# The low parts of 58 feed-forward weight tiles: an adding DMA in place of a VectorE subtraction

## The chip, the core and the metric

One core of a Trainium2 chip runs the whole program. A core has TensorE (PE, matrix products; PEld is its weight load), VectorE (DVE), ScalarE (ACT), GpSimd (POOL) and SyncE (SP). The engines run side by side, each through its own list in order, and wait for each other on semaphores. Here SP and POOL issue nearly all DMAs, and one set of 16 DMA engines carries them.

The metric is the time of one execution on the device in microseconds (us). Smaller is better.

## The reference, cut to what matters

It is one decoder layer, on 512 prompt tokens and 8 sample tokens that share all weights, in float32:

```python
h = rms_norm(x, g_pre1) * (1 + scale1) + shift1
z = h @ w_in                                # q | k | v | g | u | a | gate_r | gate_c
# retention over q, k, v (4 heads) -> ret_out ; causal convolution of u * sigmoid(a) -> conv_out
mix = (sigmoid(gr) * ret_out + sigmoid(gc) * conv_out) @ w_out
x = x + gate1 * rms_norm(mix, g_post1)
h = rms_norm(x, g_pre2) * (1 + scale2) + shift2
x = x + gate2 * rms_norm((silu(h @ w_gate) * (h @ w_up)) @ w_down, g_post2)
```

The model width is 1024 and the feed-forward width 2816, which is 22 column blocks of 128. Next to `x` the layer returns the updated retention states: 8 samples x 4 heads, each state 512 KB.

## The kernel before, in words

Activations lie with the channels on the 128 partitions and the 520 tokens along the row. A product runs in two halves of 260 tokens ("sides" 0 and 1), into one accumulator tile `acc` in PSUM, of which there are two.

**High and low parts.** Each factor of a product is split in two float32r tiles: `hi`, the rounded value, and `lo`, what the rounding left over. Three products go into the accumulator: hi x hi, hi x lo, lo x hi. A weight tile of 128x1024 (a piece, class `Piece`) thus passes through three buffers: `raw`, loaded by SP (line 89), `hi`, a rounding copy on ACT (line 168), and `lo`, the subtraction raw - hi on DVE (line 137). In `gemm_pe` each of the 8 blocks of a piece has six matmuls of 260 columns: four with `hi`, then two with `lo`. So the first use of a piece's `lo` stands behind four matmuls of its item.

**Items and their order.** The program is a fixed list of items, each with its matmuls (`pe`), what follows them on ACT and DVE (`post`) and its pieces. `Ctx.run` walks the list and writes each engine's instructions in that order. While it writes item i, it also writes the split of the pieces of the next items, so many that their planned cost reaches 10 us (`SPLIT_AHEAD`): in the feed-forward stage with both sides these are the pieces of item i+2. The load of a piece is written two pieces ahead of that (`DMA_AHEAD`). On ACT the order of one step is therefore: split of item i+2, then `post` of item i.

**Feed-forward.** For each column block f there are two items, gate and up. The `post` of gate is a Silu on ACT from `acc`. The `post` of up is a multiplication on DVE from `acc`, then the split of the product into hi (ACT) and lo (DVE). Blocks 0 to 4 (`NLAG = 5`) run one side at a time, earlier. Blocks 5 to 21 run with both sides: 17 x 2 pieces. The down projection then has 8 output blocks with three pieces each (8, 8 and 6 blocks of 128): 24 pieces.

**State updates.** Between the feed-forward items stand the last updates of the sample states (`state_unit`). One update is: on POOL, the load of the state of two updates later (line 1099); on ACT, four scaled copies (line 165, `T<-T,vsm`); on DVE, one scalar-tensor-tensor (line 150); on POOL, the store of the state (`ret_s`, line 1092), which waits for DVE. POOL issues its DMAs strictly in its own order. In the stage with both sides one update comes after about every second item: first behind the up items, and from block 15 on behind the gate items. For some samples a 512 KB load of rows (line 672) stands with it.

**Buffers.** `raw`, `hi` and `lo` tiles, the states and the activations share 45 buffers ("T4"), which are taken again in the order in which they come free.

Of the kernel before, what the change touches and what calls it, by code (L numbers as in the profile page):

```python
# [9 lines left out]
F32R = mybir.dt.float32r  # L10
I32 = mybir.dt.int32
AF = mybir.ActivationFunctionType
ALU = mybir.AluOpType
AX = mybir.AxisListType
PSUM = bass.MemoryType.PSUM
DRAM = bass.MemoryType.DRAM

P = 128
D = 1024
KT = 8  # L20
# [10 lines left out]
NF = DFF // P  # L31
# [25 lines left out]

# order of the loads at the start, and of the items of the start and of the middle (">x" splits x's weights early)
LOADS = "x0 0.1 2.0 x1 x2 x3 2.1 2.2 1.0 2.3 A0 0.0 3.0 0.2 0.3 3.2 3.1 3.3 A1 B0 U0 1.2 1.1 1.3 U1 B1"
# [9 lines left out]
NLAG = 5  # L69


class Item:
# [3 lines left out]
    def __init__(self, pe, post=None, pieces=(), cost=0.0, pre=None):  # L76
        self.pe, self.post, self.pieces, self.cost, self.pre = pe, post, list(pieces), cost, pre


class Piece:  # L80
    def __init__(self, k, src, shape, split=True):
        self.k, self.src, self.shape, self.want_split = k, src, list(shape), split
        self.raw = self.hi = self.lo = None

# [6 lines left out]
    def split(self):  # L91
        if self.want_split:
            self.hi, self.lo = self.k.split(self.raw, self.shape, late=self.k.late_w)
            self.raw = None
# [185 lines left out]
def halves(ap2d):  # L280
    return ap2d.rearrange("p (a b) -> p a b", a=2)


def emit(k, ins, outs):
# [21 lines left out]

    # modulation: quarters of the rows accumulate in four column groups of the array
    def ada_item(blk, n=2):
# [178 lines left out]
    items = []  # L487

    # start: modulation of the first norm, statistics of x
    ada = {b: ada_item(b, 1) for b in range(4)}  # L490
# [3 lines left out]

    # conv branch
    scv = k.sm([P, KT, NB], "scv")
    glu = {}
    conv = {}
# [64 lines left out]
    for j in range(KT):  # L563
# [24 lines left out]
        if j == 0:  # L588
            start = {f"{b}.{i}": it for b in range(4) for i, it in enumerate(ada[b])}
# [23 lines left out]

    # retention heads
    cos, sin = halves(csn[:, 0, :]), halves(csn[:, 1, :])
# [316 lines left out]

    # the last head's state product waits in DRAM for the end of the kernel
    def park(h):
        d = hd[h]
        kept = []
        for q in list(d["kd"]) + [q for p in range(2) for q in d["V"][p]]:
            kept.append(k._t(k.dram, [P, 4 * DK], F32R, f"park{len(kept)}"))
            nc.gpsimd.dma_start(kept[-1], q.rearrange("p a b -> p (a b)"))

        def back():
            t = []
            for i, q in enumerate(kept):
                t.append(k.t4([P, 4, DK] if i < 2 else [P, 2, DV], F32R))
                nc.gpsimd.dma_start(t[-1].rearrange("p a b -> p (a b)"), q)
            d["kd"], d["V"] = t[:2], {0: t[2:4], 1: t[4:6]}
        box["back"] = back
# [46 lines left out]

    # layer norm of the conv branch
    def ln_mean():
# [82 lines left out]

    # update of the sample states  # L1080
    def state_unit(h, b):
# [38 lines left out]

    # gates of the branches, merge
    sgr = {}
# [16 lines left out]
    last = []  # L1139
# [36 lines left out]

    # output projection, second norm
    MX = {}
# [163 lines left out]

    # feed-forward
    ACT = {}
# [25 lines left out]

    fpc = [(Piece(k, ins["w_gate"][f], [P, KT, P]), Piece(k, ins["w_up"][f], [P, KT, P])) for f in range(NF)]
    for a in range(2):
# [44 lines left out]
    def down_pieces(m):  # L1417
        return [Piece(k, ins["w_down"][m][:, 8 * i:min(NF, 8 * i + 8), :], [P, min(8, NF - 8 * i), P])
                for i in range(3)]
# [6 lines left out]
    def final(a):  # L1426
# [16 lines left out]
        return post  # L1443

    dp = [down_pieces(m) for m in range(KT)]
    items.append(Item(gains2))
    for m in range(KT - 2):
# [98 lines left out]
```

## Time and profile before

| what | value |
|---|---|
| time, median of 2 runs | 1189.4 us (1189.3 to 1189.51) |
| profiled execution: span from first to last instruction | 1188.2 us |
| what lies around the span (median less span) | 1.2 us |
| PE busy | 1165.3 us, 98% |
| DVE / ACT / POOL busy | 764.9 / 425.4 / 85.2 us |
| mean DMA rate over the span | 166 GB/s |
| granted TensorE clock, mean | 0.998 |

The profile page has no time of its own for the profiled execution besides its span. A line such as "L137 DVE" names the line of the kernel on which the instruction is recorded; many operations are recorded in one helper, so tiles and shapes tell them apart. "Idle before" is the time an engine stood still just ahead of an instruction, with what ended it. In a timeline the columns are: start, duration, engine, line, operation, tiles with sizes, count, and in brackets the idle time before. Busy time of PE is modelled, so it is read together with the chain of waits.

### The profile page before, as it was taken

The page shows a single profiled execution, that of the slowest core. Times are in us where ns is not written, and L with a number is a line of the kernel's source. Part 1 is how long each engine was busy: PE and PEld are TensorE (multiplying, and loading weights), DVE is VectorE, ACT ScalarE, POOL GpSimd, SP SyncE. Part 2 cuts the span into 40 slices and gives each one's busy share as a digit, 9 for nine tenths or more (in the row PEclk, how much of TensorE's full clock was granted, in tenths as well). Part 3 has the DMA queues.
Part 4 walks back from the last instruction along what each step waited for, and adds up shares of the span by engine and source line. Part 5 has one row for each costly group of instructions (what it writes and reads, how often), then busy time and mean ns, then how long its engine had stood idle before and what let it go on. Part 6 is the DMA issues. An engine that isn't in the chain of part 4 may idle for free.

```text
span 1188.2 us, 22500 instructions
## 1 busy us (share of the span) xinstructions
PE 1165.3 (98%) x9460; PEld 1128.4 (95%) x9460; DVE 764.9 (64%) x1475; ACT 425.4 (36%) x701; POOL 85.2 (7%) x153
## 2 busy tenths in 40 slices
PE   5999999999999999999999999999999999999997
PEld 2999999999999999999989999999999999999996
DVE  4697798999798989896545536685344443432224
ACT  3421233343233232334336335563344444332210
POOL 0000020011001100110000110100011111000000
PEclk9999999999999999999999999999999999999999
DMA  9821252244225432567554645634575564462224
GB/s 378 353 92 56 74 205 91 88 161 169 72 90 173 156 106 72 195 227 270 213 201 165 230 166 179 226 125 143 207 253 195 183 223 172 165 200 82 84 67 143
DMA packets 56885, 197.48 MB, mean 166 GB/s; under 512 B 6544, under 2 KB 8848, under 8 KB 56784
## 3 DMA queue, kind: packets, MB, share of 16 engines
q1 hardware_dynamic: 37008, 125.89, 30.2%
q0 software_dynamic: 19632, 70.12, 16.9%
q8 instruction: 74, 1.21, 0.4%
q14 instruction: 27, 0.22, 0.1%
q10 hardware_dynamic: 144, 0.04, 0.0%
HBM read 171.65 MB, written 25.32 MB: 166 GB/s over the span
## 4 chain that ended last, share of the span: by engine, by line
PE 97%; DVE 1%; DMA 1%; ACT 0%; SPq 0%; issue 0%; DVEq 0%
PE acc L207 88%; PE ps L207 7%; DVE T L137 1%; DMA T<-xT 1%; PE ps L958 1%; PE ps L844 1%; PE ps L329 0%; DVE T L150 0%; PE ps L785 0%; ACT T L165 0%; PE ps L658 0%; ACT T L168 0%; SPq L89 0%; DVEq L1542 0%; DVE ada_r L336 0%
## 5 line engine op out<-in xcount | busy, mean ns | idle before, releaser
L207 PE MATMUL acc<-T,T 128*128 128x260 f32 x8592 | 1055.8, 284 | 1.0 <-DVE T L137 0.5
L207 PEld LDWEIGHTS acc<-T,T 128*128 128x128 f32 x8592 | 1040.1, 188 | 12.0 <-issue 3.4
L137 DVE TENSOR_TENSOR T<-T,T 128x1024 fp32r<-128x1024 f32 (+8 forms) x343 | 328.2, 984 | 121.0 <-ACT T L168 77.6
L168 ACT CAST T<-T 128x1024 fp32r<-128x1024 f32 (+7 forms) x255 | 227.6, 927 | 257.2 <-DVE T L137 245.8
L137 DVE TENSOR_TENSOR T<-acc,T 128x520 f32<-128x520 f32 (+1 forms) x99 | 64.9, 669 | 158.9 <-PE acc L207 155.0
L150 DVE SCALAR_TENSOR_TENSOR T<-T,vec,T 128x511 f32<-128x511 f32 (+14 forms) x240 | 161.6, 729 | 0.0
L165 ACT ACTIVATE T<-acc 128x520 f32<-128x520 f32 (+1 forms) x98 | 50.3, 514 | 219.0 <-PE acc L207 219.0
L150 DVE SCALAR_TENSOR_TENSOR T<-T,T 128x1024 f32<-128x1024 f32 x32 | 39.2, 1225 | 53.3 <-ACT T L165 52.1
L165 ACT ACTIVATE T<-acc,GT 128x260 f32<-128x260 f32 (+1 forms) x32 | 15.2, 475 | 110.5 <-PE acc L207 100.3
L165 ACT ACTIVATE T<-T,vsm 128x256 f32<-128x256 f32 x128 | 54.2, 499 | 0.0
L207 PE MATMUL ps<-T,T 128*128 128x512 f32 (+3 forms) x264 | 51.8, 349 | 0.0
L168 ACT COPY T<-acc 128x520 f32<-128x520 f32 (+2 forms) x46 | 22.1, 481 | 73.8 <-PE acc L207 73.8
L207 PEld LDWEIGHTS ps<-T,T 128*128 128x128 f32 x264 | 42.5, 188 | 5.9
L692 DVE CUSTOM_DVE_ANT_0 T<-T,T 128x256 f32<-128x256 f32 x128 | 45.6, 419 | 0.0
L207 PE MATMUL ps<-T,cs 128*32 128x512 f32 x192 | 29.0, 647 | 11.4 <-DMA T<-w_ada 11.4
L1092 POOL DMA_DIRECT2D ret_s<-T x32 | 17.2, 537 | 255.1 <-DVE T L150 234.8
L207 PEld LDWEIGHTS ps<-T,cs 128*32 128x32 f32 x192 | 5.3, 112 | 21.5 <-issue 15.7
L137 DVE TENSOR_TENSOR T<-ps,T 128x512 fp32r<-128x512 f32 (+4 forms) x32 | 18.6, 585 | 9.3 <-ACT T L168 7.8
L150 DVE SCALAR_TENSOR_TENSOR T<-ps,vec,T 128x256 fp32r<-128x256 f32 (+1 forms) x32 | 18.5, 611 | 8.3 <-PE ps L958 7.6
L1099 POOL DMA_DIRECT2D T<-sret x32 | 16.9, 530 | 96.3 <-PE acc L207 73.2
L165 ACT ACTIVATE T<-ps,gn_b,gn_n 128x512 f32<-128x512 f32 x16 | 11.1, 779 | 32.1 <-DVE gn_b L150 23.1
L672 POOL DMA_DIRECT2D T<-rows x16 | 12.3, 770 | 142.1 <-PE acc L207 120.4
(110 smaller groups left out, 342.6 us busy)
## 6 DMA issues: line engine op xcount, KB each, us to landing
T<-w_in SPq DMA_DIRECT2D x77, 512.0 KB, 3.7
T<-sret POOLq DMA_DIRECT2D x64, 512.0 KB, 5.6
T<-w_ada SPq DMA_DIRECT2D x48, 512.0 KB, 5.4
ret_s<-T POOLq DMA_DIRECT2D x32, 512.0 KB, 4.4
T<-w_up SPq DMA_DIRECT2D x22, 512.0 KB, 4.5
T<-w_gate SPq DMA_DIRECT2D x22, 512.0 KB, 4.3
T<-rows POOLq DMA_DIRECT2D x16, 512.0 KB, 5.2
T<-w_ret_out SPq DMA_DIRECT2D x16, 512.0 KB, 3.5
```

The lines of the kernel that those rows point to most:

```text
L137: self.nc.vector.tensor_tensor(out=out, in0=a, in1=b, op=op)
L150: self.nc.vector.scalar_tensor_tensor(out=out, in0=a, scalar=s, in1=b, op0=op0, op1=op1)
L165: self.nc.scalar.activation(out, a, func, **kw)
L168: self.nc.scalar.copy(out, a)
L207: self.nc.tensor.matmul(out, lhsT=w, rhs=x, start=start, stop=stop)
L672: nc.gpsimd.dma_start(t, qk_rows[h][4 * g:4 * g + 4, i, :].unsqueeze(0).to_broadcast([P, 4, DK]))
L692: nc.vector.tensor_tensor_reduce(out=junk, in0=s0[b][:, vt, :], in1=d["qb", b // 4][:, b % 4, :], op0=ALU.mult, op1=ALU.add, scale=1.0, sc ...
L844: nc.tensor.transpose(t[:, vt * P:(vt + 1) * P], d["v"][vt // 2][:, vt % 2, jt * P:(jt + 1) * P], ident)
L958: nc.tensor.transpose(t[:, it * P:(it + 1) * P], d["y"][it // 2][:, it % 2, vt * P:(vt + 1) * P], ident)
L1092: nc.gpsimd.dma_start(outs["ret_s"][h, b], s0)
L1099: nc.gpsimd.dma_start(box2["s0"], ins["sret"][h, b])
```

## The change

A piece can now be marked `summed`. This mark is set on the gate and up pieces of blocks 5 to 21 (34) and on all 24 pieces of the down projection: 58. For such a piece ACT first writes -raw into `lo`, rounded to float32r, then the rounded copy into `hi`; then POOL issues a DMA that reads the same weights from DRAM once more and adds them onto `lo`. `lo` then holds raw less its rounded value. The subtraction on DVE is gone for these pieces. All other pieces stay as they are.

```diff
 class Piece:
-    def __init__(self, k, src, shape, split=True):
+    def __init__(self, k, src, shape, split=True, summed=False):
         self.k, self.src, self.shape, self.want_split = k, src, list(shape), split
+        self.summed = summed
         self.raw = self.hi = self.lo = None
...
     def split(self):
-        if self.want_split:
+        if self.summed:
+
+            k = self.k
+            self.hi, self.lo = k.t4(self.shape, F32R), k.t4(self.shape, F32R)
+            k.act(self.lo, self.raw, AF.Copy, scale=-1.0)
+            k.copy(self.hi, self.raw)
+            k.nc.gpsimd.dma_start(self.lo, self.src, accum_op=ALU.add)
+            self.raw = None
+        elif self.want_split:
             self.hi, self.lo = self.k.split(self.raw, self.shape, late=self.k.late_w)
             self.raw = None
...
-    fpc = [(Piece(k, ins["w_gate"][f], [P, KT, P]), Piece(k, ins["w_up"][f], [P, KT, P])) for f in range(NF)]
+    fpc = [tuple(Piece(k, ins[w][f], [P, KT, P], summed=f >= NLAG) for w in ("w_gate", "w_up")) for f in range(NF)]
...
-        return [Piece(k, ins["w_down"][m][:, 8 * i:min(NF, 8 * i + 8), :], [P, min(8, NF - 8 * i), P])
+        return [Piece(k, ins["w_down"][m][:, 8 * i:min(NF, 8 * i + 8), :], [P, min(8, NF - 8 * i), P], summed=True)
                 for i in range(3)]
```

The rest of the diff takes comments out. Lines behind line 100 stand 9 later in the changed kernel. PE's and SP's lists keep their order. On POOL, at the updates that stand near blocks 10 to 12 of the feed-forward, the list was this before (`T4_...` are buffers, those of `sret` and `ret_s` hold states):

```order
L1099 DMA T4_1427_10682<-sret 128x1024
L1092 DMA ret_s<-T4_1402_10430 128x1024
L1099 DMA T4_1438_10806<-sret 128x1024
L1092 DMA ret_s<-T4_1414_10556 128x1024
L1099 DMA T4_1451_10932<-sret 128x1024
L1092 DMA ret_s<-T4_1427_10682 128x1024
```

The same place on POOL in the changed kernel, where line 99 is the adding DMA:

```order
L1108 DMA T4_1427_10696<-sret 128x1024
L1101 DMA ret_s<-T4_1402_10440 128x1024
L99 DMA T4_1431_10708<-w_gate 128x1024
L99 DMA T4_1436_10766<-w_up 128x1024
L1108 DMA T4_1438_10822<-sret 128x1024
L1101 DMA ret_s<-T4_1414_10568 128x1024
L99 DMA T4_1442_10834<-w_gate 128x1024
L99 DMA T4_1447_10892<-w_up 128x1024
L1108 DMA T4_1451_10950<-sret 128x1024
L1101 DMA ret_s<-T4_1427_10696 128x1024
```

Between the store of one update and the load of the next now stand two adds, and the add of a gate piece is right behind a store. Further on, from block 16, where the update follows the gate item, it is the add of an up piece that stands right behind the store.

On ACT the list at the same blocks was this before (`vsm` marks the scaled copies of an update, an `acc` source the Silu, a `T2` source the hi part of the product):

```order
L165 ACTIVATE T4_1428_10684<-T4_1373_10161,vsm_40_146 128x256 x4
L168 CAST T4_1430_10693<-T4_1416_10565 128x1024
L165 ACTIVATE T2_1433_10745<-acc_1432_10696 128x520
L168 CAST T4_1435_10750<-T4_1421_10622 128x1024
L168 CAST T4_1425_10676<-T2_1433_10745 128x520
L165 ACTIVATE T4_1439_10808<-T4_1413_10554,vsm_40_146 128x256 x4
```

And on ACT after:

```order
L174 ACTIVATE T4_1428_10698<-T4_1373_10167,vsm_40_146 128x256 x4
L174 ACTIVATE T4_1431_10708<-T4_1416_10577 128x1024
L177 CAST T4_1430_10707<-T4_1416_10577 128x1024
L174 ACTIVATE T2_1433_10761<-acc_1432_10712 128x520
L174 ACTIVATE T4_1436_10766<-T4_1421_10635 128x1024
L177 CAST T4_1435_10765<-T4_1421_10635 128x1024
L177 CAST T4_1425_10691<-T2_1433_10761 128x520
L174 ACTIVATE T4_1439_10824<-T4_1413_10566,vsm_40_146 128x256 x4
```

Each weight's rounding copy has a negating copy of the same size ahead of it; nothing else moved on ACT.

## The prediction

> **What bounds the kernel now.** I read the page's busy times and its chain first, then the chain in order of time, the busy time by stage, and at last the timeline of one step of the stage that the change touches.
>
> ```profile
> span 1188.2 us, 22500 instructions
> PE 1165.3 (98%) x9460; PEld 1128.4 (95%) x9460; DVE 764.9 (64%) x1475; ACT 425.4 (36%) x701; POOL 85.2 (7%) x153
> PE 97%; DVE 1%; DMA 1%; ACT 0%; SPq 0%; issue 0%; DVEq 0%
> L207 PE MATMUL acc<-T,T 128*128 128x260 f32 x8592 | 1055.8, 284 | 1.0 <-DVE T L137 0.5 <-DVE T L150 0.4
> ```
>
> PE carries 97% of the chain. The last row is the group of all large products: ahead of 8592 matmuls PE stood 1.0 us in all, half of it for the line on which the removed subtractions stand. The chain in order of time (start, length, what) shows where the changed pieces are used:
>
> ```profile
> 877.84 280.32 PE acc L207 x2340
> ```
>
> For 280 us PE waits for nobody. The changed pieces of blocks 5 to 21 and the whole down projection lie in this stretch and the 27 us ahead of it. By stage (length, busy time of PE, PEld, DVE, ACT, POOL, clock, DMA share, GB/s), with the start of the program as the row of the highest DMA rate:
>
> ```profile
> 862.00:1045.00 183.00, 183.00 (x1528) 182.02 (x1527) 77.86 (x84) 77.70 (x135) 22.06 (x40) 1.00 0.58 197
> 1045.00:1159.00 114.00, 114.00 (x959) 114.00 (x958) 31.33 (x34) 31.66 (x61) 2.78 (x6) 1.00 0.33 105
> ...
> 0.00:30.00 30.00, 17.06 (x84) 6.88 (x84) 13.31 (x38) 10.34 (x15) 1.44 (x6) 1.00 0.96 379
> ```
>
> DVE, from which the work is taken, is busy 78 of 183 us in the gate/up stage and 31 of 114 in the down stage. So the question is not what DVE saves but whether the new path to `lo` is still in time for PE.
>
> **The change part by part.**
>
> *Removed: 58 subtractions.* The groups by shape, in the stretch from 850 to 1132 us (a piece of 6 blocks is 128x768):
>
> ```profile
> L137 DVE TENSOR_TENSOR T<-T,T 128x1024 fp32r<-128x1024 f32 x47 | 56.8, 1219 | 9.5 <-ACT T L168 6.4 <-issue 3.1
> L137 DVE TENSOR_TENSOR T<-T,T 128x768 fp32r<-128x768 f32 x7 | 6.7, 957 | 48.0 <-ACT T L168 48.0
> L168 ACT CAST T<-T 128x1024 fp32r<-128x1024 f32 x47 | 48.6, 1050 | 1.4 <-PE acc L207 0.9 <-DVE T L137 0.4
> ```
>
> 50 x 1.219 + 8 x 0.957 = 68.6 us leave DVE. None of it is on the chain: the 1.0 us of PE's idle time above is all that could come back, and it is spread over the whole kernel. I take 0.
>
> *Added on ACT: 58 negating copies.* Not shown as such; the nearest row is the rounding copy of the same tile, 1.05 us. In the gate/up stage ACT rises from 78 to about 78 + 34 x 1.05 = 113 of 183 us. One step shows what stands behind it (start, duration, engine):
>
> ```profile
> 906.74 0.70 DVE L137 TENSOR_TENSOR T<-acc,T 128x520 f32<-128x520 f32 x1 [6.22 <-PE acc L207]
> 907.35 1.82 DVE L137 TENSOR_TENSOR T<-T,T 128x1024 fp32r<-128x1024 f32 x2
> 907.47 0.63 ACT L168 CAST T<-T 128x520 fp32r<-128x520 f32 x1 [5.03 <-DVE T L137]
> 908.00 1.71 ACT L165 ACTIVATE T<-T,vsm 128x256 f32<-128x256 f32 x4
> ...
> 909.62 1.03 ACT L168 CAST T<-T 128x1024 fp32r<-128x1024 f32 x1
> 909.75 1.23 DVE L150 SCALAR_TENSOR_TENSOR T<-T,T 128x1024 f32<-128x1024 f32 x1 [0.57 <-ACT T L165]
> 910.89 1.22 DVE L137 TENSOR_TENSOR T<-T,T 128x1024 fp32r<-128x1024 f32 x1
> 911.26 0.54 POOL L1092 DMA_DIRECT2D ret_s<-T  x1 [9.78 <-DVE T L150]
> 911.80 0.53 POOL L1099 DMA_DIRECT2D T<-sret  x1
> ...
> 912.44 0.60 ACT L165 ACTIVATE T<-acc 128x520 f32<-128x520 f32 x1 [1.79 <-PE acc L207]
> ...
> 918.26 0.70 DVE L137 TENSOR_TENSOR T<-acc,T 128x520 f32<-128x520 f32 x1 [6.16 <-PE acc L207]
> ```
>
> An up item ends at 906.74 and the next one at 918.26: 11.52 us for two items, 5.76 each, 0.12 a matmul. The copy at 909.62 is that of the gate piece used from 918.26 on. With a negation ahead of it, ACT is done at 909.62 + 2 x 1.04 = 911.7, before the Silu at 912.44; nothing is late. The negation behind the Silu ends near 914, and ACT has nothing more to do before 919. So ACT's part costs 0; its cover is the 1.79 us of idle time ahead of the Silu, of which 1.05 go.
>
> *Moved: the end of `lo`.* Before, `lo` of that gate piece was done by the subtraction at 910.89 + 1.22 = 912.1, 6.1 us ahead of PE. Now the add is issued by POOL, and there the order of the list counts: it stands behind the store `ret_s`, which waits for DVE's update and so is issued at 911.26 to 911.80. What is queued behind the add on POOL is the up piece's add and the next state's load; that load is needed two updates later and has room. From the end of the up item the add begins at 911.80 - 906.74 = 5.06 us. It has to land 11.52 us after that end, plus the four matmuls that need only `hi`: 11.52 + 0.48 = 12.0. That leaves 6.94 us from issue to landing. Seven gate pieces in a row (blocks 10 to 16) stand like this.
>
> From block 15 on the update follows the gate item:
>
> ```profile
> 1015.95 0.60 ACT L165 ACTIVATE T<-acc 128x520 f32<-128x520 f32 x1 [3.40 <-PE acc L207]
> 1016.45 1.69 ACT L165 ACTIVATE T<-T,vsm 128x256 f32<-128x256 f32 x4
> ...
> 1018.17 1.23 DVE L150 SCALAR_TENSOR_TENSOR T<-T,T 128x1024 f32<-128x1024 f32 x1 [4.37 <-ACT T L165]
> 1019.69 0.54 POOL L1092 DMA_DIRECT2D ret_s<-T  x1 [6.82 <-DVE T L150]
> ...
> 1027.46 0.60 ACT L165 ACTIVATE T<-acc 128x520 f32<-128x520 f32 x1 [3.42 <-PE acc L207]
> ```
>
> The gate item ends at 1015.95, the store's issue at 1020.23, so the add of an up piece begins after 4.28 us and has 12.0 - 4.28 = 7.72. Six up pieces and the first middle piece of the down projection: seven. The last update follows the last up item, and behind its store stands one more down piece, with the gate pieces' 6.94. Adds without a store ahead start 2 to 3 us earlier and have 9 us and more. Blocks 6 to 9 have stores too, but there PE has other work of about a microsecond between items; I count them at 0.
>
> *The price of the add, A.* No adding DMA is in the trace. The nearest row is the state load: POOL's queue, 512 KB from DRAM, issued right behind the same store. Its landings in this stage, what POOL's queue moved there (packets, MB, share of the 16 engines over 183 us), and POOL's issue times, for the row load (more descriptors) and the state load:
>
> ```profile
> L1099 POOL DMA_DIRECT2D T<-sret x17: 528/528/531, 862.5 to 1023.9; - x17
> ...
> DMA to landing us min/median/max: 3.6/6.3/8.8
> ...
> q0 software_dynamic: 5616, 20.45, 31.7%
> ...
> L1099 POOL DMA_DIRECT2D T<-sret x17 | 9.0, 529 | 13.7 <-DVE T L137 7.2 <-DMA ret_s<-T 5.2 <-PE acc L207 0.9
> L672 POOL DMA_DIRECT2D T<-rows x4 | 3.0, 761 | 1.7 <-PE acc L207 1.7
> ```
>
> Low end: 3.6, the fastest load. High end: twice the median, 12.6, as if the read of the old `lo` were a second load behind the first. I take the median and one more pass over 512 KB: 0.317 x 183 = 58 us for 20.45 MB is 1.5 us for 0.524 MB, so A = 6.3 + 1.5 = 7.8. POOL's issue may take 0.76 instead of 0.53 us; I add 0.23 to the start of each.
>
> *The sum.* A stall ahead of one piece also gives the next add that much more time, so in a row of pieces half of the excess stays. Gates and the last down piece: 8 x (0.23 + 7.8 - 6.94) / 2 = 4.4 us. Ups: 7 x (0.23 + 7.8 - 7.72) / 2 = 1.1. Together 5.5. With A = 3.6 it is 0; with the largest state load, 8.8, it is 8 x 1.05 + 7 x 0.66 = 13; with 12.6 it is 8 x 2.95 + 7 x 2.56 = 41.
>
> *The rest of the down stage.* The copies of three pieces stand behind each output block's five evacuations:
>
> ```profile
> 1060.59 0.48 ACT L165 ACTIVATE T<-acc,GT 128x260 f32<-128x260 f32 x1 [10.25 <-issue]
> ...
> 1061.90 2.76 ACT L168 CAST T<-T 128x768 fp32r<-128x768 f32 x3
> 1062.80 3.31 DVE L137 TENSOR_TENSOR T<-T,T 128x768 fp32r<-128x768 f32 x3 [10.55 <-ACT T L168]
> ...
> 1076.34 0.48 ACT L165 ACTIVATE T<-acc,GT 128x260 f32<-128x260 f32 x1 [11.68 <-PE acc L207]
> ```
>
> Of the 15.75 us from one block to the next, the first of the three is used after 2 x 5.76 = 11.5 us. Its add is issued near 1062.9 and would land at 1070.7, needed at 1072.1; the two others have more. Cost 0.
>
> The span of the profiled execution is 1188.2, the median of the runs 1189.4, so 1.2 us lie around it. 1188.2 + 5.5 + 1.2 = 1194.9: I say 1195.
>
> **The rivals.** The line for a difference that a measurement of this kernel is taken to tell is 2%, 23.8 us.
>
> *The add is slow (slower).* One mechanism, at the gate and up pieces behind a store: with A from issue to landing the stall is 4 x (A - 6.71) + 3.5 x (A - 7.49), which reaches 23.8 at A = 10.2. For it: the read of the old tile, the rounding at the end, and a store of 512 KB just ahead in the same queue. Against it: the slowest of 17 loads in this place took 8.8. At A = 12.6 the time is 1189.4 + 41 = 1230.
>
> *The DMA engines fill up (slower).* In the stage they are busy 0.58. Two adds per 11.52 us at 1.5 us each are 0.26, at two passes each 0.52, so 0.84 or 1.10; in the latter case the 183 us stretch by 10%, 18 us and what the waits add: 1207 to 1215. Against it: 197 GB/s plus 2 x 0.524 MB / 11.52 us = 91 is 288, below the 379 of the start. [...]
>
> *PE gains (faster).* Only 1.0 us of PE's waiting for DVE is there in the products, so the best is 1188.4. That the subtractions stay, or are replaced by other work on DVE, is excluded: the built program has 58 fewer of them there.
>
> **How the numbers follow.** The forecast (A between 3.6 and 9, 1189 to 1203): 0.66. The slow add: 0.20, of which 0.12 over 23.8 us. Full DMA engines: 0.12, of which 0.07 over it. Faster: 0.02, and over 2% 0.01 at most. The range from 1187.5 to 1216 leaves out the outer part of the two slower rivals, about 0.16, and little below. Slower by over 2%: 0.19; faster 0.01; within 2%: 0.80.
>
> **What would show it.** Right: PE idle ahead of some `acc` matmuls, put down to the DMAs of `w_gate` and `w_up` and no longer to none; landings of the adds near 8 us; DVE lower by 69 us, ACT higher by 60; the span from 1045 us on longer by nothing. Wrong: landings above 10, a DMA share near 1 between 862 and 1045, waits of PE for pieces of the down projection, or a Silu that waits for ACT's negations and so keeps an accumulator from PE.

## The result, and the profile after

The changed kernel takes 1217.36 us (median of 2 runs, 1215.03 to 1219.69) against 1189.4 before: a ratio of 1.0234, with a 95% interval of 1.021 to 1.0259. It is slower by 28 us, where 5.5 us were forecast, and it lies just above the upper end of the range, 1216.

The page of the kernel after has these lines (span, busy times, queues, memory traffic, shares of the chain, the group of all large products):

```profile
span 1217.9 us, 22596 instructions
PE 1175.0 (96%) x9460; PEld 1135.6 (93%) x9460; DVE 701.3 (58%) x1417; ACT 478.7 (39%) x759; POOL 136.6 (11%) x211
q0 software_dynamic: 27984, 99.48, 29.6%
HBM read 201.01 MB, written 25.32 MB: 186 GB/s over the span
PE 77%; issue 13%; DMA 4%; POOL 3%; DVE 2%; ACT 1%; SPq 0%; POOLq 0%; DVEq 0%
L216 PE MATMUL acc<-T,T 128*128 128x260 f32 x8592 | 1065.5, 285 | 21.5 <-DMA T<-w_up 8.2
```

The work moved as it was meant to: DVE is 64 us lower, ACT 53 higher, and the 29.4 MB of the 58 weights are read a second time. The last line says where the time went, in two parts. PE stands still for 21.5 us ahead of the large products, where it was 1.0. And the same 8592 matmuls take 1065.5 us, where they took 1055.8. That is 20.5 + 9.7 = 30.2 us, and the span has grown by 29.7.

The stalls one by one (PE's timeline after; start, length of the run of matmuls that follows, in brackets the idle time ahead of it and what ended it):

```profile
869.81 7.93 PE L216 MATMUL acc<-T,T 128*128 128x260 f32 x44 [4.67 <-DMA T<-w_up]
892.56 6.01 PE L216 MATMUL acc<-T,T 128*128 128x260 f32 x48 [1.22 <-DMA T<-w_gate]
900.85 17.50 PE L216 MATMUL acc<-T,T 128*128 128x260 f32 x144 [2.27 <-DMA T<-w_up]
920.52 23.32 PE L216 MATMUL acc<-T,T 128*128 128x260 f32 x192 [2.18 <-DMA T<-w_gate]
944.57 11.78 PE L216 MATMUL acc<-T,T 128*128 128x260 f32 x96 [0.73 <-DMA T<-w_gate]
958.65 23.24 PE L216 MATMUL acc<-T,T 128*128 128x260 f32 x192 [2.30 <-DMA T<-w_gate]
983.65 19.06 PE L216 MATMUL acc<-T,T 128*128 128x260 f32 x144 [1.77 <-DMA T<-w_gate]
1003.20 23.33 PE L216 MATMUL acc<-T,T 128*128 128x260 f32 x192 [0.48 <-DMA T<-w_up]
1026.95 23.31 PE L216 MATMUL acc<-T,T 128*128 128x260 f32 x192 [0.43 <-DMA T<-w_up]
1050.62 23.31 PE L216 MATMUL acc<-T,T 128*128 128x260 f32 x192 [0.35 <-DMA T<-w_up]
1077.89 110.08 PE L216 MATMUL acc<-T,T 128*128 128x260 f32 x896 [3.96 <-DMA T<-w_down]
```

They add up to 20.4 us and fall into four places. Up to 901 us, on the up piece of block 6 and both pieces of block 8: 4.67 + 1.22 + 2.27 = 8.2. Four of the seven gates behind a store, those of blocks 10, 12, 13 and 15: 2.18 + 0.73 + 2.30 + 1.77 = 7.0; a stall gives the next add more time. Every second of the six ups behind a store, blocks 16, 18 and 20: 1.3. And 3.96 on the first middle piece of the down projection. From there on PE runs 110 us without a stop.

The second part, the slower matmuls, is seen in windows of 2 us behind a stall (length, PE busy and matmuls, PEld, DVE, ACT, POOL, granted clock, DMA share, GB/s):

```profile
870.00:872.00 2.00, 2.00 (x10) 2.00 (x11) 0.00 (x0) 0.21 (x1) 2.00 (x4) 0.50 0.94 295
872.00:874.00 2.00, 2.00 (x11) 2.00 (x11) 0.00 (x0) 0.00 (x0) 0.63 (x2) 0.50 1.07 283
874.00:876.00 2.00, 2.00 (x14) 2.00 (x13) 0.00 (x0) 0.00 (x0) 0.00 (x0) 0.71 1.03 299
876.00:878.00 2.00, 2.00 (x19) 1.69 (x21) 0.23 (x1) 0.00 (x0) 0.00 (x0) 1.00 1.07 379
```

PE is as busy as before, but for 6 us it does 10 to 14 matmuls in 2 us where 19 are usual: the granted clock is 0.50 to 0.71. Behind the stall that ends at 1077.89 it is the same; behind the one that ends at 983.65 it is so for 4 us. (The share of the DMA engines, the column behind the clock, can read a little over 1 in a short window, here up to 1.07.)

The stage rows show the engines that the adds pass through (the same columns; the adds' landing time stands below):

```profile
862.00:1045.00 183.00, 166.95 (x1341) 164.09 (x1340) 41.45 (x50) 98.00 (x154) 47.69 (x68) 0.97 0.96 271
1072.00:1186.00 114.00, 110.04 (x897) 109.83 (x897) 4.10 (x8) 47.12 (x77) 20.91 (x26) 0.97 0.82 188
```

```profile
DMA to landing us min/median/max: 4.8/7.6/13.7
```

The share of the DMA engines has gone from 0.58 to 0.96. The adds' median of 7.6 us is what the forecast took (7.8); their spread reaches 13.7.

### The profile page after: what moved, and what is told of

The parts are those of the page before. It is cut to its first block, busy times and chain, and to the rows that moved or that the text cites. A ratio compares the mean times of both kernels' runs of the same rounds, so it can differ in the third digit from the quotient of the medians.

```text
span 1217.9 us, 22596 instructions
## 1 busy us (share of the span) xinstructions
PE 1175.0 (96%) x9460; PEld 1135.6 (93%) x9460; DVE 701.3 (58%) x1417; ACT 478.7 (39%) x759; POOL 136.6 (11%) x211
## 3 DMA queue, kind: packets, MB, share of 16 engines
q1 hardware_dynamic: 37008, 125.89, 29.6%
q0 software_dynamic: 27984, 99.48, 29.6%
## 4 chain that ended last, share of the span: by engine, by line
PE 77%; issue 13%; DMA 4%; POOL 3%; DVE 2%; ACT 1%; SPq 0%; POOLq 0%; DVEq 0%
PE acc L216 68%; PE ps L216 7%; POOL T L99 1%; DVE T L146 1%; POOL T L1108 1%; DMA T<-w_down 1%; DMA T<-sret 1%; DMA T<-w_gate 1%; DVE T L159 1%; DMA T<-w_up 1%; PE ps L967 1%; PE ps L853 1%; DMA T<-xT 1%; POOL ret_s L1101 1%; ACT T L174 0%
## 5 line engine op out<-in xcount | busy, mean ns | idle before, releaser
L216 PE MATMUL acc<-T,T 128*128 128x260 f32 x8592 | 1065.5, 285 | 21.5 <-DMA T<-w_up 8.2
L146 DVE TENSOR_TENSOR T<-T,T 128x1024 fp32r<-128x1024 f32 (+10 forms) x285 | 262.4, 944 | 153.0 <-ACT T L174 116.5
L174 ACT ACTIVATE T<-T 128x1024 fp32r<-128x1024 f32 (+3 forms) x74 | 73.6, 996 | 14.3 <-DVE T L146 11.7
L99 POOL DMA_DIRECT2D T<-w_down x24 | 20.4, 864 | 87.4 <-ACT T L174 87.4
L99 POOL DMA_DIRECT2D T<-w_gate x17 | 15.0, 884 | 107.0 <-ACT T L174 106.2
L1108 POOL DMA_DIRECT2D T<-sret x32 | 23.2, 737 | 11.6 <-DVE T L146 10.2
```

The costliest lines, as they stand in the source:

```text
L99: k.nc.gpsimd.dma_start(self.lo, self.src, accum_op=ALU.add)
L146: self.nc.vector.tensor_tensor(out=out, in0=a, in1=b, op=op)
L174: self.nc.scalar.activation(out, a, func, **kw)
L216: self.nc.tensor.matmul(out, lhsT=w, rhs=x, start=start, stop=stop)
L1108: nc.gpsimd.dma_start(box2["s0"], ins["sret"][h, b])
```

## The experiments

Two theories stand against each other. *Position* (P): an add is issued so late in its place, behind a store on POOL, that it has about 7 us until PE needs it, and takes about that long. *Full engines* (F): the 16 DMA engines are at their limit, and everything that passes through them is late. In the expectation on the state loads the blocks of the early stalls are numbered wrongly: "block 7" there is the up piece of block 6, and the 5.7 us on "blocks 8 and 9" are the 1.22 and 2.27 us of block 8 and the 2.18 of block 10. Each kernel below is the changed kernel with the edit shown, if nothing else is said. Each time is the median of 4 to 10 executions, and each ratio is to the kernel before, with its 95% interval.

**Only the down pieces summed.** The gate and up pieces go back to subtractions.

```diff
-    fpc = [tuple(Piece(k, ins[w][f], [P, KT, P], summed=f >= NLAG) for w in ("w_gate", "w_up")) for f in range(NF)]
+    fpc = [tuple(Piece(k, ins[w][f], [P, KT, P], summed=False) for w in ("w_gate", "w_up")) for f in range(NF)]
```

> Only the 24 pieces of the down projection are formed by adding DMAs; the 34 gate and up pieces keep the subtraction on VectorE. In the changed kernel the time from the end of the last up item to the end grew by 6.8 us. If that comes from the down adds themselves, the time is about 1196. If it comes from the gate and up adds that still fill the DMA engines when the down projection begins (theory F, full engines), or from their place behind the last state stores in a crowded queue (theory P, position), it is gone here: 1189 to 1191.

1195.32 us, ratio 1.0045 (1.003 to 1.006). There is one stall. Its row, POOL's rows for the add that PE waits for, and the windows around it:

```profile
1053.79 109.04 PE L216 MATMUL acc<-T,T 128*128 128x260 f32 x896 [3.91 <-DMA T<-w_down]
```

```profile
1042.40 0.55 POOL L1101 DMA_DIRECT2D ret_s<-T  x1 [6.09 <-DVE T L159]
1042.94 0.89 POOL L99 DMA_DIRECT2D T<-w_down  x1
```

```profile
1054.00:1056.00 2.00, 2.00 (x13) 2.00 (x13) 0.00 (x0) 0.00 (x0) 0.00 (x0) 0.68 1.11 299
1056.00:1058.00 2.00, 2.00 (x12) 2.00 (x11) 0.00 (x0) 0.00 (x0) 0.00 (x0) 0.50 1.07 214
...
1044.00:1056.00 12.00, 8.09 (x63) 7.88 (x62) 2.47 (x4) 7.48 (x11) 3.16 (x4) 0.95 1.03 303
```

The time is the 1196 that was expected if the down adds themselves are at fault. The add stands behind a store, is issued at 1042.94 and has landed at 1053.79: 10.85 us, in a stretch in which the engines are full (1.03). Here both theories are at work at once. In the kernel before, the engines were nearly as full in the same 12 us, and PE did not stop:

```profile
1044.00:1056.00 12.00, 12.00 (x102) 12.00 (x102) 6.95 (x8) 4.87 (x8) 0.53 (x1) 1.00 0.92 315
```

The other 23 adds of the down projection stop nothing.

**Only the gates summed**; the down pieces have `summed=False`.

```diff
-    fpc = [tuple(Piece(k, ins[w][f], [P, KT, P], summed=f >= NLAG) for w in ("w_gate", "w_up")) for f in range(NF)]
+    fpc = [tuple(Piece(k, ins[w][f], [P, KT, P], summed=f >= NLAG and w == "w_gate") for w in ("w_gate", "w_up")) for f in range(NF)]
```

> Only the 17 gate pieces are formed by adding DMAs. Theory P (position: the add of a gate piece stands behind the store of the state and so comes late whatever the engines do): the stalls ahead of the gate pieces stay, some 7 to 8 us, with a few us of slow clock behind them: 1197 to 1200. Theory F (the DMA engines are full: 106 us of work in the stage of 183 us, and 2.75 us for each add): 106 + 17 x 2.75 = 153 of 183 us, so the stalls are mostly gone: 1189 to 1193.

1202.13 us, 1.0108 (1.0081 to 1.0134), a little above what theory P expected and well above theory F. The profiled execution was the slowest of the four, 1206.73 us. In it PE waits 10.5 us for gates, at a DMA share of 0.77:

```profile
862.00:1045.00 183.00, 172.72 (x1381) 170.49 (x1380) 56.99 (x65) 87.00 (x143) 34.85 (x54) 0.96 0.77 234
```

The adds land in 5.6 to 11.1 us, median 7.3. With a quarter of the DMA engines' time free, the gates stop PE about as much as in the changed kernel (8.2 us there, blocks 8 to 15). Full engines alone don't explain it.

**Plain loads in the adds' place.** The same DMAs without the addition; `lo` then holds the rounded weight itself.

```diff
-            k.nc.gpsimd.dma_start(self.lo, self.src, accum_op=ALU.add)
+            k.nc.gpsimd.dma_start(self.lo, self.src)
```

> All 58 adding DMAs become plain rounding loads of the same bytes into the same tiles, with the same issue, the same waits and the same ACT work (so lo holds the weight itself: this part of the computation is changed). It tells the price of adding against loading. Theory F: a load takes 1.5 us of the engines instead of 2.75, so 106 + 34 x 1.5 = 157 of 183 us, and the time falls to 1190 to 1197. Theory P: the landing comes only about 1.2 us sooner, half of which is left in a row of pieces: 1204 to 1212.

1201.01 us, 1.009 (1.0073 to 1.0107), between the two expectations. Landing falls to 3.4/5.7/9.1 and the share to 0.82; the stalls sum to 8 us. POOL's queue line gives the price for the engines:

```profile
q0 software_dynamic: 27984, 99.48, 24.3%
```

24.3% of a span of 1199.5 us is 291.5 us, where the kernel before has 16.9% of 1188.2, 200.8. The 58 plain loads are 90.7 us, 1.56 each. The 58 adds are 29.6% of 1217.9 less the same, 159.7 us: 2.75 each. (These are means over 50 pieces of 512 KB and 8 of 384 KB. They take it that the other DMAs cost what they cost before; SP's queue, the same 125.89 MB in all three kernels, speaks for it with 358.8 us before, 360.5 with the adds and 352.7 with the plain loads.) For the same packets and bytes an add keeps the engines 1.76 times as long, where the rival of full engines took two passes.

**The adds read the raw tile on the chip, not DRAM.**

```diff
-            k.nc.gpsimd.dma_start(self.lo, self.src, accum_op=ALU.add)
+            k.nc.gpsimd.dma_start(self.lo, self.raw, accum_op=ALU.add)
```

> The changed kernel, but the adds read the weights from the raw tile on the chip and not from DRAM once more, so HBM moves 29 MB less; the raw tile stays taken until the add has landed. If reading DRAM a second time is what makes the adds late, the landings get shorter by 1 us or more and the time falls to 1196 to 1208. If it is the DMA engines' own work on an add, the time stays: 1211 to 1222. If the raw tiles that are held longer make loads late, it rises above that.

1217.15 us, 1.0232 (1.0211 to 1.0253): no different from the changed kernel.

```profile
q0 software_dynamic: 27984, 99.48, 29.1%
HBM read 171.65 MB, written 25.32 MB: 162 GB/s over the span
```

The DRAM traffic is back at that of before (171.65 MB read there too), the engines' share stays, and the adds land in 7.2 us (median) in place of 7.6, less than the 1 us that a cheaper read was to give. The second read of the weights is not the cause; the add itself is what the engines spend their time on (29.1% of the span here, 29.6% with the source in DRAM, 24.3% with the plain loads).

**The store issued behind the next add.** POOL's order at an update becomes add, store, for the updates at blocks 7 to 20.

```diff
-                nc.gpsimd.dma_start(outs["ret_s"][h, b], s0)
+                k.puts.append(lambda: nc.gpsimd.dma_start(outs["ret_s"][h, b], s0))
...
             k.nc.gpsimd.dma_start(self.lo, self.src, accum_op=ALU.add)
+            k.put()
```

> The changed kernel, but on POOL each state store of the gate and up stage is issued behind the next add and no longer ahead of it; the bytes are the same. Theory P: the adds start 0.9 to 1.3 us sooner and have no store ahead of them in the queue, so at least half of the stalls go: 1198 to 1206. Theory F: the engines have the same work, the time stays: 1213 to 1220.

1207.39 us, 1.0147 (1.0132 to 1.0162), at a DMA share of 0.98. The idle time ahead of the products falls from 21.5 to 12.3. The time is just above what theory P expected; a third of the loss goes by position alone. The two large stalls, at block 6 (3.98) and in the down projection (3.07), stay, but the edit did not reach them: there the store still stands ahead of the add (store at 861.85 and add at 862.38, store at 1055.30 and add at 1055.85). At all other places together the stalls fall from 11.7 to 4.2 us, more than the half that theory P asked for.

**No state loads in these updates.** DVE scales the copies instead of the state, so that the loads, but not the stores, leave POOL's queue; the states are then not updated.

```diff
-                k.stt(s0, s0, GAMMA[h], kv, ALU.mult, ALU.add)
+                k.stt(s0, kv, GAMMA[h], kv, ALU.mult, ALU.add)
-            nc.gpsimd.dma_start(box2["s0"], ins["sret"][h, b])
```

> The changed kernel without the loads of the sample states in the updates (VectorE takes the scaled copies in place of the old state, so this part of the computation is changed); stores, adds and their order on POOL stay. This takes 22 transfers of 512 KB out of the gate and up stage, 1.5 us of all engines each, 33 of some 200 us. Theory F: the stalls fall to less than half, 1193 to 1203. Theory P: the load stands behind the adds of its own step, so the adds land nearly as before, 1208 to 1218.

1205.32 us, 1.0121 (1.0099 to 1.0144), share 0.86. It settles little: it takes work from the engines and at the same time the wait for the loads from POOL's order. But one row fell out of the pattern. The first stall, at block 6, was 0.81 us and no longer 4.67.

**Only blocks 5 to 9 summed**; the down pieces have `summed=False`.

```diff
-    fpc = [tuple(Piece(k, ins[w][f], [P, KT, P], summed=f >= NLAG) for w in ("w_gate", "w_up")) for f in range(NF)]
+    fpc = [tuple(Piece(k, ins[w][f], [P, KT, P], summed=NLAG <= f < 10) for w in ("w_gate", "w_up")) for f in range(NF)]
```

> Only the ten gate and up pieces of blocks 5 to 9 are formed by adding DMAs. In the changed kernel PE stood 8.2 us ahead of such pieces, where the prediction counted nothing. If these stalls belong to their own place (a state update with each item, so that store, add and load follow each other in POOL's queue), they stay and bring slow clock with them: 1198 to 1203. If they come from what the later adds do to the queue, or were chance, they are gone: 1189 to 1192.

1199.14 us, 1.0085 (1.0067 to 1.0104). These ten adds lose 9.7 us by themselves, a third of the whole. The prediction had put them at 0.

**First all products with `hi`, then those with `lo`.** In a summed piece 32 matmuls, 3.9 us, now stand ahead of the first use of `lo`, not 4. The sum is the same.

```diff
+            def low(kt):
+                for a in sides:
+                    xh, _ = xin(S, kt, a)
+                    k.mm(bank(t, a), wsrc(kt)[1], xh, False, kt == (kts[-1] if last is None else last))
...
+                if not hifirst:
+                    low(kt)
+            if hifirst:
+                for kt in kts:
+                    low(kt)
```

> The changed kernel with one thing else: in the items of the 58 pieces PE runs all matmuls with the high part first and those with the low part at the end, so that the first use of the low part stands behind 32 matmuls (3.9 us) and not behind four (0.5 us). DMAs, their places and their bytes are the same. Theory P (each add lands a little late for its place; stalls of up to 4.7 us and a slow clock behind them): stalls of up to 3.4 us vanish, and with them most slow clock: 1189 to 1194. Theory F (the 16 engines have more work than time in the gate and up stage): the engines fall behind step by step, more room moves a stall but does not remove it: above 1205.

1198.14 us, 1.0071 (1.0055 to 1.0087): between the two expectations, 4 us above that of theory P and 7 below that of theory F. This run separates the theories best. The stage and the adds' landing:

```profile
862.00:1045.00 183.00, 178.66 (x1462) 176.35 (x1462) 44.66 (x53) 107.02 (x166) 50.84 (x72) 0.98 1.01 292
```

```profile
DMA to landing us min/median/max: 4.8/8.6/14.3
```

The engines are fuller than in the changed kernel (1.01) and the adds slower (8.6), and yet two thirds of the 28 us are gone, for 3.4 us more room per piece. What is left is 3.28 us at block 6, 1.06 at block 8 and 0.35 in the down projection.

**The same, and only from block 10 on** (48 adds).

```diff
-    fpc = [tuple(Piece(k, ins[w][f], [P, KT, P], summed=f >= NLAG) for w in ("w_gate", "w_up")) for f in range(NF)]
+    fpc = [tuple(Piece(k, ins[w][f], [P, KT, P], summed=f >= 10) for w in ("w_gate", "w_up")) for f in range(NF)]
```

> Both moves at once: the products with hi of all blocks of a summed piece come ahead of those with lo (3.9 us of matmuls ahead of the first use of lo, not 0.48), and only blocks 10 to 21 and the down projection are summed (48 adds). Position: all adds have 10 us and more, so 1189 to 1191.5, neither loss nor gain although 48 subtractions have left DVE. Full engines: the share is that of the changed kernel from block 10 on, so above 1199.

1191.26 us, 1.0017 (1.0007 to 1.0026). Its group of large products:

```profile
L216 PE MATMUL acc<-T,T 128*128 128x260 f32 x8592 | 1056.8, 284 | 1.7 <-DVE T L146 0.5 <-DVE T L159 0.4 <-DMA T<-w_gate 0.4
```

48 subtractions have left DVE, the DMA share is 0.94 in the stage, and PE waits 0.7 us more than in the kernel before. Nothing is gained: the work on DVE was never in PE's way.

**Splits and adds one item earlier**, from the first summed item on, so that an add behind a store has 5.76 us more.

```diff
+            ahead = 1.6 * split_ahead if any(p.summed for p in it.pieces) else split_ahead
-            while j < len(items) and t < split_ahead and not items[j].hold:
+            while j < len(items) and t < ahead and not items[j].hold:
```

> The changed kernel with the weights from block 5 on split (and added to) one item earlier, 5.76 us more between an add's issue and its use; the same 58 adds and the same work for the DMA engines. Position (the adds land a little late for their place): the budget behind a store grows from 6.9 to 12.7 us, above nearly all landings (median 7.6, largest 13.7): 1190 to 1196, stalls of PE below 4 us in all. Full engines: the work is the same, so above 1205.

1203.74 us, 1.0118 (1.0104 to 1.0132): outside both expectations. Its stalls:

```profile
858.61 5.53 PE L216 MATMUL acc<-T,T 128*128 128x260 f32 x44 [0.15 <-DMA T<-w_gate]
869.36 8.08 PE L216 MATMUL acc<-T,T 128*128 128x260 f32 x44 [4.30 <-DMA T<-w_up]
892.74 137.98 PE L216 MATMUL acc<-T,T 128*128 128x260 f32 x1148 [1.70 <-DMA T<-w_gate]
1032.12 11.77 PE L216 MATMUL acc<-T,T 128*128 128x260 f32 x96 [1.40 <-ACT T L174]
1045.29 125.39 PE L216 MATMUL acc<-T,T 128*128 128x260 f32 x1044 [1.40 <-ACT T L174]
```

On POOL the adds up to that of block 8's gate stand where they stood; from there on they come one item earlier, and no add stops PE any more, at a DMA share of 0.99. What the edit does not reach is block 6: 4.30 us and the low clock behind it (0.50 from 870 to 875 us). New are two waits of 1.40 us for ACT. Its rows ahead of the first:

```profile
1026.54 1.06 ACT L174 ACTIVATE T<-T 128x1024 fp32r<-128x1024 f32 x1 [2.87 <-DMA ret_s<-T]
1030.52 1.04 ACT L177 CAST T<-T 128x1024 fp32r<-128x1024 f32 x1 [2.92 <-PE acc L216]
1031.47 0.60 ACT L174 ACTIVATE T<-acc 128x520 f32<-128x520 f32 x1
```

The negation waits for a store and the rounding copy for PE, as I read it for buffers that these still read. The Silu behind both comes late and keeps its accumulator from PE.

**The control: the kernel before, split one item earlier.** The same line in the kernel with subtractions.

> Control: the kernel before, subtractions and all, with the same splitting one item earlier. Both theories: 1188 to 1192. If it is slower, the buffers that the earlier splits hold are what costs, and the run with the adds is to be read against this one.

1189.73 us, 1.0003 (0.9994 to 1.0012). Splitting earlier costs nothing by itself.

**Fillers in the stall.** Only the down pieces summed, as in the first experiment, and ahead of the middle piece 32 extra matmuls.

```diff
+                if m == 0 and c == 1:
+                    fill = k.pps()
+                    for _ in range(32):
+                        k.mm(fill[:, :HT], pc.hi[:, 0, :], xin(ACT, 8, 0)[0], True, True)
```

> Only the 24 down pieces summed, and ahead of the item of the first block's middle piece 32 matmuls of 260 columns into an unused tile (3.8 us), where the kernel without them stood still for 3.91 us and then ran at a clock of 0.5 to 0.7 for some 8 us. If the stall causes the low clock: the fillers fill the stall, the clock stays at 1.0, and the time is 1.5 to 2 us below that kernel's 1195.3, so 1193 to 1194. If the low clock has another cause (the load on the chip at that place): 1195 to 1196.

1193.07 us, 1.0031 (1.0019 to 1.0042), as expected from a clock that the stall brings down. (The low clock in the kernel without fillers lasted 4 us, at 0.68 and 0.50 in its windows above, and not the 8 of the expectation.) The interval overlaps that of the kernel without fillers, so the windows carry the point:

```profile
1054.00:1056.00 2.00, 2.00 (x19) 2.00 (x18) 0.00 (x0) 0.00 (x0) 0.16 (x1) 1.00 1.01 395
1056.00:1058.00 2.00, 2.00 (x19) 2.00 (x18) 0.00 (x0) 0.00 (x0) 0.00 (x0) 1.00 1.08 280
```

With PE kept at work the clock stays at 1.00 at the same place and the same DMA load (1.01 and 1.08, where it was 1.11 and 1.07 at 0.68 and 0.50). The low clock there comes from the standing still.

**The first state loads ahead of the adds.** What was left was block 6. On POOL, before and after:

```profile
830.57 0.53 POOL L1099 DMA_DIRECT2D T<-sret  x1 [70.03 <-PE acc L207]
...
836.20 0.53 POOL L1099 DMA_DIRECT2D T<-sret  x1 [1.60 <-PE acc L207]
855.67 0.54 POOL L1092 DMA_DIRECT2D ret_s<-T  x1 [18.94 <-DVE T L150]
```

```profile
851.85 0.84 POOL L99 DMA_DIRECT2D T<-w_gate  x1 [10.36 <-ACT T L174]
852.38 0.87 POOL L1108 DMA_DIRECT2D T<-sret  x1
...
861.76 0.54 POOL L1101 DMA_DIRECT2D ret_s<-T  x1 [6.66 <-DVE T L159]
862.29 0.92 POOL L99 DMA_DIRECT2D T<-w_up  x1
```

Before, nothing in POOL's list waited for ACT here; POOL waited only for PE, ran ahead and issued the first state loads of this stage at 831 to 836 us. After, an add that waits for ACT stands ahead of them, and they go out from 852 on. Then follows a chain: the load is late, so the update on DVE is late, which waits for `sret` (854.15 before):

```profile
860.24 1.22 DVE L159 SCALAR_TENSOR_TENSOR T<-T,T 128x1024 f32<-128x1024 f32 x1 [14.65 <-DMA T<-sret]
```

So the store is late, and so is the add of block 6's up piece, at 862.29. PE needs it some 3 us later and gets it at 869.81. The edit writes these three loads four items earlier; the third is loaded once more at its old place, one transfer of 512 KB too many:

```diff
-            for n in (i, i + 1, i + 2) if i == start else (i + 2,):
+            for n in (i, i + 1, i + 2) if i == start and not start else (i + 2,):
...
+    items.insert(len(items) - 4, Item(lambda: [us[n][0]() for n in (nst, nst + 1, nst + 2)]))
```

> The changed kernel with the first three state loads of the feed-forward stage written four items earlier, so that on POOL they stand ahead of the adds of blocks 5 and 6 and no longer behind adds that wait for ACT. Everything else is as it was, the work of the DMA engines too. POOL's order (late loads make late updates, late stores and so late adds): block 7's stall of 4.67 us goes, and with it part of the 5.7 us on blocks 8 and 9 and some 3 us of low clock: 1205 to 1212. The add's own time or full engines: a stall above 3 us stays at block 7, and the time is above 1214.

1212.95 us, 1.0189 (1.0171 to 1.0207), 4.4 us less than the changed kernel (whose two executions lie 4.7 us apart) and just above what was expected. Two of its rows:

```profile
878.97 6.04 PE L216 MATMUL acc<-T,T 128*128 128x260 f32 x48 [0.37 <-DMA T<-w_up]
887.46 25.01 PE L216 MATMUL acc<-T,T 128*128 128x260 f32 x192 [2.45 <-DMA T<-w_gate]
```

The 4.67 us ahead of block 6's up piece are gone (the rows are those of block 7's up and block 8's gate), and the add goes out at 856.56 in place of 862.29, so POOL's order was their cause. The idle time of the whole group falls from 21.5 to 16.1. Not all is kept: the gate of block 8, whose place behind its store is unchanged, now stops PE by 2.45 us in place of 1.22.

**Both: state loads ahead, and all splits and adds one item earlier.** The state loads as in the last edit, and for the splits:

```diff
+            ahead = 1.6 * split_ahead if any(p.summed for n in items[i:i + 5] for p in n.pieces) else split_ahead
-            while j < len(items) and t < split_ahead and not items[j].hold:
+            while j < len(items) and t < ahead and not items[j].hold:
```

> The same, and all splits and adds from block 5 on one item earlier. Position and POOL's order: no stall above 2 us is left, 1190 to 1197, with the DMA share between 862 and 1045 us at 0.95 or more. Full engines: above 1200.

1195.98 us, 1.0052 (1.0035 to 1.0068), as position and POOL's order expected. The stage and the group of large products:

```profile
862.00:1045.00 183.00, 178.19 (x1475) 175.97 (x1474) 41.80 (x50) 103.72 (x159) 48.46 (x69) 1.00 0.99 286
```

```profile
L216 PE MATMUL acc<-T,T 128*128 128x260 f32 x8592 | 1057.9, 284 | 6.3 <-ACT T L174 3.3 <-DMA T<-w_up 1.2 <-DMA T<-w_gate 0.8
```

All 58 adds are in, the DMA engines are at 0.99, the landings range from 5.3 to 16.7 us, and PE waits 2.0 us for adds in place of 20. 21 of the 28 us of loss are gone by order alone. What is left is mostly the 3.3 us of waiting for ACT and 2.1 us more of busy time of the matmuls, at a clock of 1.00 in the stage.

No kernel here is faster than the one before.

## Why the prediction was right and wrong

**Right: that the subtractions were worth nothing.** 0 was taken for the 68.6 us that leave DVE. The kernel that sums 48 pieces and leaves PE hardly a stall (1.7 us of waiting for 1.0) is at 1.0017 of the time before.

**Right: the mechanism, the price of the add, and the rows of gates and ups.** A was taken at 7.8 us, and the median is 7.6. Here luck helped: the sum was 6.3 for a load and 1.5 for one more pass, and the runs have 5.7 for a plain load in the same place and 1.9 more for the add. An example: the gate's add that was to start 5.06 + 0.23 us behind the end of an up item, at 906.40 in this trace, starts 5.11 us behind it, at 911.51. Of the forecast's 4.4 us, 3.8 were for the seven gates; they cost 7.0. The six ups were 0.9 and cost 1.3. POOL's issue was taken at 0.76 us, and its row is 0.85 to 0.88 long (medians).

**The step that failed: "I count them at 0" for blocks 6 to 9.** Blocks 6 and 8 cost 8.2 us of standing still. The reason given was that PE has other work there between the items. That is so, but it looked at how far away the need is, and not at when POOL comes to the add. An earlier sentence said of the state load behind the adds that it "has room". The first three state loads POOL had issued some 20 us earlier before the change, waiting for PE alone, and an add that waits for ACT ended that. The prediction named what is queued behind the new wait, but priced it by its place in the list and not by the time at which it had been issued: 831 us before, 852 after. With these loads ahead again, 3.1 of the 8.2 us are left (0.32 and 0.37 at block 7, 2.45 at block 8): that part belongs to the adds' own place behind their stores, which the prediction had not worked out for these blocks.

**Mis-sized: the first middle piece of the down projection.** It was one of the seven "ups" with 7.72 us, at a cost of 0.16, and cost 3.96. Its add took 10.9 us, in a stretch in which SP issues a row of down weights: the engines were at 0.92 there before, and are at 1.03 with the adds of the down pieces alone. That this crowd is what makes the add slow is likely, but no run takes those loads away. The mean over the whole down stage, 0.33, the only DMA share that the prediction has for it, does not show the crowd.

**Mis-sized: one median for all adds.** Half of the excess of a median was taken, so 7.8 against 6.94 gave 0.5 us a gate. Landings from 4.8 to 13.7 give stalls of up to 2.3 us in the same rows: an add that lands early gives nothing back, one that lands late costs all of its excess.

**Missing: the clock.** 9.7 us of the loss are matmuls that take longer. Around the stalls that end at 869.81, 983.65 and 1077.89 the clock is 0.50 for 3.4 to 6.8 us; counted in matmuls that are missing from the windows of 2 us (22, 13 and 23 of 0.12 us) it is 7.0 of the 9.7. The other 2.7 us are not shown to be the clock: the kernel with both moves has 2.1 us of the same at a clock of 1.00. The forecast had no such term. A stall of 3.9 to 4.7 us costs 5.5 to 7.3 us in all.

So 21.7 of the profile's 30.2 us stand in places where the forecast had almost nothing: 8.2 in the early blocks, 3.8 in the down projection, 9.7 in the longer matmuls.

**The rivals.** *The add is slow* did not come about: it wanted a landing of 10.2 us, and the median is 7.6. *The DMA engines fill up* was half right. The share did go to 0.96. The two passes that it took for an add are shown by no run; measured are 2.75 us an add against 1.56 a plain load, 1.76 times. But the time that it gave, 18 us by engines that can't keep up, is not where the loss came from: at 1.01 and at 0.99 the kernels with other orders lose 8.7 and 6.6 us. Full engines may widen the landings (5.6 to 11.1 us at a share of 0.77, 4.8 to 13.7 at 0.96), but no run changes the share alone. How much of the stalls this makes is not settled: plain loads in the same place, which keep the engines 1.56 and not 2.75 us, lose 11.6 us and not 28, but they also land 1.9 us sooner by themselves.

**The signs.** Of those named, the waits for `w_gate` and `w_up`, the landing near 8, the lower DVE (64 of 69 us) and the higher ACT (53 of 60) came about, and of the signs against it the share near 1 and a wait for a piece of the down projection. A Silu behind ACT's negations that keeps an accumulator from PE was seen only with the splits moved earlier.

## What to carry to other kernels

Work that leaves an engine which nobody waits for was worth nothing here (48 subtractions gone, ratio 1.0017); what counted was whether the new path to the same tile was still in time, item by item, with the slowest of its transfers (13.7 us) and not the median (7.6). An instruction that waits, put into a queue that ran ahead before, ended that running ahead (831 us became 852): look up when the instructions behind it were issued before the change, since what they had in hand is lost. And a DMA that comes late for its place is mended first by its place (an earlier issue, or a later first use), which here gave back 19 and 21 of 28 us with the DMA engines as full as before.

## What the runs showed of the hardware

- The 58 adding DMAs (494 KB in the mean) keep the 16 DMA engines for 2.75 us each, plain ones in the same place for 1.56; with the source on the chip instead of in DRAM it is 29.1% of 1216.6 less 200.8, over 58, so 2.64. To landing they took 7.6 us against 5.7 (medians). POOL's issue of an add is a row of 0.84 to 0.92 us for gates, where a plain load's is 0.53 to 0.55; but the row behind it begins 0.53 to 0.59 us after its start, so POOL is hardly held longer.
- A stall of PE can cost twice: the 3.91 us in the down projection cost 5.5, the 4.67 us at block 6 cost 7.3. After stalls of 1.77 and 3.91 us the granted clock was 0.50 for 3.4 us, around stalls of 3.96 and 4.67 us for 6.8 us; after 2.18, 2.27 and 2.30 us it stayed at 1.00, so the length alone didn't decide it.
- In windows of 0.25 us the clock of the changed kernel falls at 868.34, 984.39 and 1076.55 and stays at 0.50 for 6.83, 3.41 and 6.83 us. The falls are 116.05 and 92.16 us apart, 34 and 27 times the shortest of these stretches. What decides which stall brings the clock down is not shown: the 1.77 us did, the 2.30 us did not.
- With state loads ahead and all adds one item earlier, two adds per pair of items and all other traffic kept the engines at 0.99 for 183 us, and PE waited 2.0 us for adds. A share near 1 in itself stopped nobody for long who had asked early enough.
